# A hybrid decoder layer on one core: the gated unit of the second half woven into the first output projection, the last RWKV group split in place, and pools whose tiles wait by bytes

## The chip, the cores and the metric

The kernel runs on one core of a Trainium2 chip. The metric is the device time of one execution in microseconds. Three runs of the kernel before took 1652.79, 1653.51 and 1653.67 us; their median is 1653.51 us. One further execution was recorded by the hardware profiler, and every row quoted below is from it.

## The reference, cut to what matters

One layer of a trunk with 1024 tokens and 1024 channels, in float32. The token mixer has two branches, an RWKV-7 recurrence (8 heads of 64) and an S5 state space with a gated unit (GLU) behind it; each is projected to the model's width, gated and summed, and the sum goes through one output projection and a norm. A convolutional feed-forward part follows.

```python
h = rms_norm(x, g_mix_pre)
proj = h @ w_in                                   # RWKV columns | S5 input | two gates
gates = sigmoid(proj[..., -2048:] + b_gate)
y = wkv7_scan(...)                                # sequential over tokens
y = (group_norm(y) * lnx_w + lnx_b + bonus) * g   # RWKV branch
s = gelu(s5(u)); s = s * sigmoid(s @ w_glu + b_glu)   # S5 branch with its gated unit
mixed = (g_rwkv * (y @ w_branch_rwkv) + g_s5 * (s @ w_branch_s5)) @ w_out
x = x + rms_norm(mixed, g_mix_post)               # post norm
f = (gelu(conv(h2 @ w_gate)) * conv(h2 @ w_val)) @ w_down     # h2 = rms_norm(x, g_ffn_pre)
x = x + rms_norm(f, g_ffn_post)
```

## The kernel before

**Layout.** Everything is held transposed: channels on the 128 partitions, tokens along the row. The 1024 tokens are worked as two halves of 512 (`th` 0 and 1). A float32 product is made of three matmuls: each operand is split into a rounded high part and a rest (`split`, `split_half`, `load_w`), and `mm3_steps` issues high x high, high x low, low x high for each 128 channels of depth. Those three matmuls are called a k-step here. A weight tile comes from DRAM into one of two landing buffers (`wf`), ScalarE rounds it (`wh`, line 155) and VectorE subtracts (`wl`, line 156); four pairs are kept.

**Order.** TensorE runs in the order in which the program emits its work. The other engines' instructions are placed by Tile, a scheduler that simulates the program ahead of time and goes by priorities. The emission is planned by `drive`: it holds *lanes*, generators that yield a cost and a time to wait (`T_CH`, `T_LN`, `T_RS`, `T_N5` and so on are such waits in model microseconds), and a list `fill` of further generators that give TensorE work while the lanes wait. So the recurrence, whose steps are short and depend on one another, is a lane; projections and gate tiles are filler. Filler has the priority HPW, above the lane's HP2. `self.pause` stops the filler, `self.mark` says where `drain` shall stop.

**The recurrence.** It runs in four groups: (half 0, channel rows 0 and 1), (half 0, rows 2 and 3), (half 1, rows 0 and 1), (half 1, rows 2 and 3). For each, `chain_lane` runs `rwkv_nat`, `rwkv_level`, `rwkv_chain` (eight chunks; line 814 reads the state S, line 825 evacuates UV, line 835 updates S) and `rwkv_out`. `rwkv_out` norms the result on VectorE (lines 845 to 855), transposes it (line 861), applies weight and bias (line 863), fetches the bonus and the gate factor through the SP queue (line 867), applies them (line 868) and stores the result to the DRAM tensor YR (line 869).

**Around its end.** After the second group the filler gets `merge` (branch projections and gates of half 0) and `outproj(0)` (output projection of half 0: eight tiles of eight k-steps, with squares accumulated, lines 1174 to 1179). When the fourth group begins it also gets `merge_s5`: first the S5 outputs of half 1 are read and split, then `glu_tile` makes the four tiles of the gated unit (four k-steps each; evictions at lines 1041, 1026, 1042, 230, 231), and then eight gate tiles project them (`gate`, line 1052). Each gate tile reads its gate tensor GT through SP (line 1049). These eight gate tiles come after the recurrence.

Then `mix_out` begins with new pools. `merge_rk` reads the four rows of YR back through SP (line 1126), splits them and makes eight gate tiles (lines 1052, 1133, 230, 231), and `outproj(1)` follows. Beside them runs the lane `mid_norms(0)`: sum of squares of the first projection by TensorE (line 244), inverse root by twelve tiny VectorE operations (lines 264 and 135 to 140), spreading it over the partitions by TensorE (line 270), then the post norm on VectorE (lines 1153, 1154, 258) with x read through SP (line 1145), and 40 model microseconds later its own sum of squares.

**Pools.** On-chip buffers come from pools that are opened and closed as the program goes on; a pool that is opened later lies on bytes of pools that were closed. In this version all tiles of the new pool wait for every user of the pools whose bytes it lies on. Such changes are between S5 and RWKV (near 265 us), between the recurrence and `mix_out` (near 846 us), and before, inside and after the feed-forward part (near 965, 1065 and 1400 us).

Of the kernel before, what the change touches and what calls it, by code (L numbers as in the profile page):

```python
# [9 lines left out]
F32 = mybir.dt.float32  # L10
# [60 lines left out]
class Kern:  # L71
# [175 lines left out]
    def tm(self):  # L247
        return self.nrm.tile([128, 512], F32, tag="Tm", name=self.nm("tm"), bufs=NTM)
# [55 lines left out]
    def s5_setup(self):  # L304
# [4 lines left out]
        with self.tc.tile_pool(name="s5tmp", bufs=1) as pool:  # L309
# [528 lines left out]
    def rwkv_out(self, d):  # L838
# [3 lines left out]
        o = slice(th * 512, th * 512 + 512)  # L842
        yn = d["yn"].rearrange("p c u h i -> p (c u h) i")
# [13 lines left out]
        for u in range(2):  # L857
# [187 lines left out]
    def gate(self, j, m, th, br, t, out):  # L1045
# [3 lines left out]
        nc.sync.dma_start(t, self.GT[8 * j + m][:, th * 512:th * 512 + 512])  # L1049
# [46 lines left out]

    def merge_s5(self, first):

        s8 = (128, 8, 64)

        slots = self.slots
        xs = []
        for b in range(4):
            y = self.s5_y(self.et(s8), b, 1)
            xs.append(slots("ex", b))
            self.s5_split(*xs[b], y)
        br = []
        for m in range(4):
            br.append(slots("eb", m))
            yield from self.glu_tile(m, xs, self.et(), lambda: self.s5_y(self.et(s8), m, 1), br[m])  # L1110
        for m in range(NK):
# [6 lines left out]
            yield from self.gate(1, m, 1, br, self.et(), first[m])  # L1118

    def merge_rk(self, first, mg):  # L1120

        nc = self.nc
        br = []
        for k in range(4):
            y = self.t2()
            nc.sync.dma_start(y, self.YR[k][:, 512:1024])
            br.append([self.t2(F32R), self.t2(F32R)])
            self.split(*br[k], y)
        yield 0
        for m in range(NK):  # L1130
            t = self.t2()
            yield from self.gate(0, m, 1, br, t, t)
# [4 lines left out]
    def post_norm(self, src, ss, th, gain, resid, store, squares=None):  # L1137
# [9 lines left out]
        y = self.rstd(ss, 1e-6, 1.0 / D)  # L1147
        yield 0, T_RS
# [17 lines left out]
    def outproj(self, th, mg, mx):  # L1166

        nc, hp = self.nc, self.hp[th]
        for m in range(NK):
            w = self.load_w(self.a["w_out"][m])  # L1170
            ps = self.gmp()
# [6 lines left out]
            if m:  # L1178
                nc.vector.tensor_tensor(sq, sq, self.acc[th], ALU.add)
# [665 lines left out]
```

## Time and profile before

| | us |
|---|---|
| median of three runs | 1653.51 |
| lowest, highest | 1652.79, 1653.67 |
| span of the profiled execution | 1650.5 |
| TensorE busy in it | 1556.1 |
| VectorE busy in it | 1128.4 |
| ScalarE busy in it | 700.1 |

The profiled execution's own device time is not on its page; only its span is, from the first to the last instruction. The median of the runs lies 3.0 us above the span, so that much is taken to lie around it. Times in the rows count from the start of the span. A row of the timeline gives start, length, engine, line, operation, output and inputs, and in brackets how long the engine had been idle and what ended that. Matmuls overlap: a length of 0.39 us stands for a step of about 0.23. The granted clock is 1.00 at full speed and 0.50 when the chip halves TensorE's clock.

### The profile page before, as it was taken

The page shows a single profiled execution, that of the slowest core. Times are in us where ns is not written, and L with a number is a line of the kernel's source. Part 1 is how long each engine was busy: PE and PEld are TensorE (multiplying, and loading weights), DVE is VectorE, ACT ScalarE, POOL GpSimd, SP SyncE. Part 2 cuts the span into 40 slices and gives each one's busy share as a digit, 9 for nine tenths or more (in the row PEclk, how much of TensorE's full clock was granted, in tenths as well). Part 3 has the DMA queues.
Part 4 walks back from the last instruction along what each step waited for, and adds up shares of the span by engine and source line. Part 5 has one row for each costly group of instructions (what it writes and reads, how often), then busy time and mean ns, then how long its engine had stood idle before and what let it go on. Part 6 is the DMA issues. An engine that isn't in the chain of part 4 may idle for free.

```text
span 1650.5 us, 22688 instructions
## 1 busy us (share of the span) xinstructions
PE 1556.1 (94%) x8372; PEld 1252.4 (76%) x8372; DVE 1128.4 (68%) x2035; ACT 700.1 (42%) x1069; POOL 134.7 (8%) x190
## 2 busy tenths in 40 slices
PE   5899899899999999989999899999999999999995
PEld 4688787687787787767777688788888888788774
DVE  6898764554364365595378668977777777788667
ACT  4345443133243243546444445544444444443451
POOL 1100001312112112110000000000000000000000
PEclk9899999998997998999999899999999999999998
DMA  5344244333333334554167554322222223963632
GB/s 174 86 142 148 78 134 142 100 110 109 90 121 104 90 119 149 149 147 128 53 189 251 159 159 144 132 89 77 89 77 85 94 78 132 316 221 99 212 97 102
DMA packets 132382, 213.63 MB, mean 129 GB/s; under 512 B 38144, under 2 KB 44288, under 8 KB 132272
## 3 DMA queue, kind: packets, MB, share of 16 engines
q1 hardware_dynamic: 124208, 188.32, 36.4%
q0 software_dynamic: 6912, 21.77, 4.5%
q10 hardware_dynamic: 1152, 2.10, 0.3%
q8 instruction: 66, 1.08, 0.3%
q14 instruction: 44, 0.36, 0.1%
HBM read 156.56 MB, written 53.48 MB: 127 GB/s over the span
## 4 chain that ended last, share of the span: by engine, by line
PE 51%; DVE 8%; DMA 5%; issue 2%; ACT 1%; SPq 0%; DVEq 0%; POOL 0%; ACTq 0%
PE gm L171 5%; PE rp L1295 4%; PE rp L1296 4%; PE rp L1297 4%; PE gm L172 4%; PE gm L173 4%; DMA st<-in_w_down_dram 2%; PE mm L1295 2%; PE mm L1296 2%; PE mm L1297 2%; PE d L1470 2%; PE d L1471 2%; PE d L1469 2%; PE ch L171 1%; PE ch L172 1%
## 5 line engine op out<-in xcount | busy, mean ns | idle before, releaser
L171 PE MATMUL gm<-hh,wh 128*128 128x512 f32 x688 | 301.2, 438 | 7.6 <-ACT hh L225 3.7
L172 PE MATMUL gm<-hl,wh 128*128 128x512 f32 x688 | 278.3, 405 | 4.6 <-DVE hl L226 3.7
L173 PE MATMUL gm<-hh,wl 128*128 128x512 f32 x688 | 277.5, 403 | 0.0
L156 DVE TENSOR_TENSOR wl<-wf,wh 128x512 fp32r<-128x512 f32 x179 | 123.1, 689 | 131.1 <-ACT wh L155 129.4
L155 ACT CAST wh<-wf 128x512 fp32r<-128x512 f32 x179 | 110.9, 620 | 207.6 <-PE gm L172 125.1
L171 PEld LDWEIGHTS gm<-hh,wh 128*128 128x128 f32 x688 | 133.7, 194 | 44.4 <-ACT hh L225 5.7
L172 PEld LDWEIGHTS gm<-hl,wh 128*128 128x128 f32 x688 | 134.5, 195 | 31.7 <-DVE hl L226 6.8
L173 PEld LDWEIGHTS gm<-hh,wl 128*128 128x128 f32 x688 | 134.0, 195 | 29.7
L1470 PE MATMUL d<-xl,wh 128*128 128x512 f32 x308 | 120.8, 392 | 6.4 <-DVE xl L226 6.4
L1469 PE MATMUL d<-xh,wh 128*128 128x512 f32 x308 | 120.8, 392 | 2.1 <-ACT xh L225 2.1
L1471 PE MATMUL d<-xh,wl 128*128 128x512 f32 x308 | 120.6, 392 | 0.0
L1295 PE MATMUL rp<-t,h 128*128 128x512 f32 x216 | 84.4, 391 | 1.8 <-ACT p L1309 1.4
L1297 PE MATMUL rp<-t,l 128*128 128x512 f32 x216 | 84.2, 390 | 0.5 <-DVE l L226 0.5
L1296 PE MATMUL rp<-t,h 128*128 128x512 f32 x216 | 84.1, 389 | 0.0
L1470 PEld LDWEIGHTS d<-xl,wh 128*128 128x128 f32 x308 | 58.2, 189 | 20.2 <-DVE xl L226 8.1
L1469 PEld LDWEIGHTS d<-xh,wh 128*128 128x128 f32 x308 | 58.2, 189 | 14.5 <-ACT xh L225 2.4
L1471 PEld LDWEIGHTS d<-xh,wl 128*128 128x128 f32 x308 | 58.1, 189 | 12.1
L225 ACT CAST h<-r 128x1024 fp32r<-128x1024 f32 x34 | 35.9, 1055 | 61.1 <-PE rp L1296 32.5
L226 DVE TENSOR_TENSOR l<-r,h 128x1024 fp32r<-128x1024 f32 x34 | 41.7, 1225 | 29.2 <-ACT h L225 27.7
L1316 DVE SCALAR_TENSOR_TENSOR y<-zv,vecs,y 128x1023 f32<-128x1023 f32 (+1 forms) x36 | 46.1, 1280 | 8.6 <-ACT y L1314 8.6
L1295 PEld LDWEIGHTS rp<-t,h 128*128 128x128 f32 x216 | 40.5, 188 | 11.4 <-ACT p L1309 2.2
L1297 PEld LDWEIGHTS rp<-t,l 128*128 128x128 f32 x216 | 40.5, 188 | 9.5 <-DVE l L226 1.0
(435 smaller groups left out, 3372.5 us busy)
## 6 DMA issues: line engine op xcount, KB each, us to landing
r<-in_w_up_dram SPq DMA_DIRECT2D x36, 512.0 KB, 3.6
wf<-in_w_in_dram SPq DMA_DIRECT2D x68, 256.0 KB, 3.1
st<-in_w_down_dram SPq DMA_DIRECT2D x55, 256.0 KB, 4.2
st<-ACT SPq DMA_DIRECT2D x44, 256.0 KB, 4.8
wf<-in_w_up_dram SPq DMA_DIRECT2D x36, 256.0 KB, 2.8
ACT<-y POOLq DMA_DIRECT2D x18, 512.0 KB, 2.9
GT<-ev SPq DMA_DIRECT2D x32, 256.0 KB, 2.2
wf<-in_w_br_dram SPq DMA_DIRECT2D x32, 256.0 KB, 3.0
```

The source lines that it names most:

```text
L155: nc.scalar.copy(h[:, :n], f[:, :n])
L156: nc.vector.tensor_tensor(l[:, :n], f[:, :n], h[:, :n].bitcast(F32), ALU.subtract)
L171: mm(ps, a, xh[k], start=k == 0, stop=False)
L172: mm(ps, a, xl[k], start=False, stop=False)
L173: mm(ps, b, xh[k], start=False, stop=k == n - 1)
L1295: mm(ps, wh[:, c], xh, start=first and k == 0, stop=False, skip_group_check=True)
L1296: mm(ps, wh[:, c], xl, start=False, stop=False, skip_group_check=True)
L1297: mm(ps, wl[:, c], xh, start=False, stop=k == 3, skip_group_check=True)
L1316: V.scalar_tensor_tensor(y[:, lag:], z[:, 0:1024 - lag], self.vec(nme, i), y[:, lag:], ALU.mult, ALU.add)
L1469: mm(ps, wh[:, c], xh[:, x], start=start, stop=False, skip_group_check=True)
L1470: mm(ps, wh[:, c], xl[:, x], start=False, stop=False, skip_group_check=True)
L1471: mm(ps, wl[:, c], xh[:, x], start=False, stop=stop, skip_group_check=True)
```

## The change

- **Gated unit.** `merge_s5` loses its first part. `s5_glu` builds five generators (the inputs, and four tiles), and `out_glu`, which takes the place of `outproj(0)` in the filler, runs them between the projection's tiles: inputs and first tile after tile 3, then one after tiles 4, 5 and 7.
- **Post norm 0.** `out_glu` ends with the sum of squares and the inverse root. `mid_norms(0)` starts at the spread. For half 1 the order stays, except that x is now requested after the inverse root.
- **Last group.** In the fourth group `rwkv_out` requests the four factor tiles at its start, through the POOL queue, and splits its result straight into the operands of `merge_rk` instead of storing it to YR. `merge_rk` reads only rows 0 and 1 back, through POOL.
- **Gates.** For half 1 the gate tensors GT are read through the POOL queue.
- **Pools.** Every on-chip pool gets `reuse_waits="tile"`: a tile waits only for earlier users of its own bytes (in PSUM, of its own bank). The pools `y1p` and `nrt` are placed ahead of `nrm`, `Tm` moves to `nrt`, and NT2B goes from 25 to 15 buffers.

```diff
 def rwkv_out(self, d):
+        final = th == 1 and d["g"] == 1
+        ts = []
+        def factors(u):
+            r = []
+            for src in (d["bv"][u], self.TG[2 * d["g"] + u][:, o]):
+                t = self.tg("ld", NLD)
+                (G if final else nc.sync).dma_start(t, src)
+                r.append(t)
+            return r
+        if final:
+            ts = [factors(u) for u in range(2)]
...
-            for src, op in ((d["bv"][u], ALU.add), (self.TG[p][:, o], ALU.mult)):
-                t = self.tg("ld", NLD)
-                nc.sync.dma_start(t, src)
+            for t, op in zip(ts[u] if final else factors(u), (ALU.add, ALU.mult)):
                 V.tensor_tensor(y1, y1, t, op)
-            nc.sync.dma_start(self.YR[p][:, o], y1)
+            if final:
+                self.br[p] = self.pair(1, p)
+                self.split(*self.br[p], y1)
+            else:
+                nc.sync.dma_start(self.YR[p][:, o], y1)
 def gate(self, j, m, th, br, t, out):
-        nc.sync.dma_start(t, self.GT[8 * j + m][:, th * 512:th * 512 + 512])
+        (nc.gpsimd if th else nc.sync).dma_start(t, self.GT[8 * j + m][:, th * 512:th * 512 + 512])
+    def s5_inputs(self, xs):
+        for b in range(4):
+            y = self.s5_y(self.et(s8), b, 1)
+            xs.append(self.slots("ex", b))
+            self.s5_split(*xs[b], y)
+        yield 0
+    def s5_glu(self):
+        s8, xs = (128, 8, 64), []
+        self.br5 = [None] * 4
+        def tile(m):
+            self.br5[m] = self.slots("eb", m)
+            yield from self.glu_tile(m, xs, self.et(), lambda: self.s5_y(self.et(s8), m, 1), self.br5[m])
+        return [self.s5_inputs(xs)] + [tile(m) for m in range(4)]
+    def out_glu(self, mg):
+        for m in range(NK):
+            yield from self.outproj_tile(0, m, mg, self.mx0)
+            if self.glu and m == 3:
+                yield from self.glu.pop(0)
+            if self.glu and m in (3, 4, 5, 7):
+                yield from self.glu.pop(0)
+        ss = self.rp()
+        self.sumsq(ss, self.acc[0], True)
+        self.y0 = self.rstd(ss, 1e-6, 1.0 / D)
+        yield 0.8
 def merge_s5(self, first):
...
+        while self.glu:
+            yield from self.glu.pop(0)
...
 def merge_rk(self, first, mg):
-        for k in range(4):
+        for k in range(2):
             y = self.t2()
-            nc.sync.dma_start(y, self.YR[k][:, 512:1024])
-            br.append([self.t2(F32R), self.t2(F32R)])
-            self.split(*br[k], y)
+            nc.gpsimd.dma_start(y, self.YR[k][:, 512:1024])
+            self.br[k] = self.pair(1, k)
+            self.split(*self.br[k], y)
 def mid_norms(self, th, mx):
-        yield 0, T_N0
+        if th:
+            yield 0, T_N0
+            ss = self.rp()
+            self.sumsq(ss, self.acc[th], True)
+            yield 0.8, 0.5
+            y = self.rstd(ss, 1e-6, 1.0 / D)
+            yield 0, T_RS
+        else:
+            y = self.y0
         ss = self.rp()
-        self.sumsq(ss, self.acc[th], True)
-        yield 0.8, 0.5
-        ss, s0 = self.rp(), ss
 def build(self):
-        with tc.tile_pool(name="const", bufs=1) as self.const, ...
+        with tc.tile_pool(reuse_waits="tile", name="const", bufs=1) as self.const, ...
 def chain_lane(self, mg):
+                self.first, self.br = [], [None] * 4
+                self.glu = self.s5_glu()
...
-                self.fill += [self.merge(mg), self.outproj(0, mg, self.mx0)]
+                self.fill += [self.merge(mg), self.out_glu(mg)]
-NT2B = 25
+NT2B = 15
```

`outproj_tile` is the body of `outproj` for one tile, and `outproj(1)` calls it eight times.

More of the change, by code (lines that the diff above doesn't have):

```diff
@@ L308, in s5_setup @@
         self.s5 = s = {}
-        with self.tc.tile_pool(name="s5tmp", bufs=1) as pool:
+        with self.tc.tile_pool(reuse_waits="tile", name="s5tmp", bufs=1) as pool:
             def sm(n=32, dt=F32):
@@ L1135, in merge_rk, with post_norm @@
             self.split_half(*mg[m], t)
-    def post_norm(self, src, ss, th, gain, resid, store, squares=None):
+    def post_norm(self, src, y, th, gain, resid, store, squares=None):
         nc = self.nc
```

96 lines of the change are left out of this document (44 added, 52 removed).

## The prediction

> **What bounds the kernel now.** I read the page first, then the busy table in stretches of 10 us, then TensorE's timeline where it sat idle, then the chain of waits and the queues around those places.
>
> ```profile
> span 1650.5 us, 22688 instructions
> PE 1556.1 (94%) x8372; PEld 1252.4 (76%) x8372; DVE 1128.4 (68%) x2035; ACT 700.1 (42%) x1069; POOL 134.7 (8%) x190
> ```
>
> ```profile
> 780.00:790.00 10.00, 10.00 (x83) 7.40 (x82) 3.26 (x8) 4.79 (x12) 0.00 (x0) 1.00 0.16 52
> ...
> 840.00:850.00 10.00, 7.74 (x32) 5.44 (x31) 8.17 (x12) 7.58 (x14) 0.00 (x0) 1.00 0.87 247
> ...
> 845.30:961.30 116.00, 103.77 (x419) 81.94 (x418) 81.57 (x146) 46.76 (x81) 0.00 (x0) 0.90 0.63 197
> ```
>
> The columns are the stretch, its length, busy PE, PEld, DVE, ACT, POOL, the granted clock, DMA share, GB/s. TensorE is the bound: full before the recurrence ends (780 to 790), with holes after it. From 845.3 to 961.3 it is idle 116 - 103.8 = 12.2 us, and a mean clock of 0.90 means 0.10 x 2 x 116 = 23 us at half speed, so up to 11.6 us more are lost.
>
> The same loss counted from the work:
>
> ```profile
> 845.28 0.39 PE L173 MATMUL gm<-e,wl 128*128 128x512 f32 x1
> 883.63 0.79 PE L171 MATMUL mm<-t,wh 128*128 128x512 f32 x1 [3.31 <-ACT t L225]
> 895.70 0.39 PE L171 MATMUL mm<-t,wh 128*128 128x512 f32 x1
> 901.14 0.39 PE L171 MATMUL mm<-t,wh 128*128 128x512 f32 x1
> 915.22 0.80 PE L171 MATMUL mm<-t,wh 128*128 128x512 f32 x1 [3.61 <-ACT t L230]
> 918.62 0.80 PE L171 MATMUL mm<-t,wh 128*128 128x512 f32 x1 [1.39 <-ACT t L230]
> 961.14 0.39 PE L171 MATMUL mm<-hh,wh 128*128 128x512 f32 x1
> 963.86 0.95 PE L244 MATMUL rp<-ones,sq 128*128 128x1 f32 x8
> ```
>
> 895.70 and 901.14 are eight k-steps (three matmuls each) apart: 0.68 us a step. The last gated unit's matmul starts at 845.28, the second output projection is over at 961.14. Between them stand 16 gate tiles of 4 steps, 8 projection tiles of 8, two sums of squares and two spreads of about 0.9 us: 128 x 0.68 + 3.6 = 90.6 us of 115.5. So 23 to 25 us are lost; I use 24. What ended the waits:
>
> ```profile
> 857.35 3.07 DMA YR<-ld
> 872.07 4.82 DMA wf<-in_w_br_dram
> 878.74 4.20 DMA t<-YR
> 911.07 5.40 DMA t<-GT
> ```
>
> The last RWKV result goes out to YR and comes back (line 1126), the last reload issued only at 878.74, because SP issues in order and weights and x stand ahead of it. The last gate tile t<-GT is issued at 911.07 for the same reason, when the projection already waits for it.
>
> **The change, part by part.**
>
> *Group split in place.* It removes two stores and two reloads of YR, and brings the bonus and gate factors early. The wait of 3.31 us goes, with its half-speed stretch. Two splits of rows 2 and 3 (about 0.7 us each on VectorE) move ahead of 846. They write buffers that the first projection still reads, so they wait for its last step, about 843 in the new order; nothing needs them before the ninth gate tile, some 22 us later.
>
> *Gates on the POOL queue.* Sixteen loads leave SP. POOL is idle there (0.00 in each row above), and in the second half nothing but the two YR reloads and the four factor loads shares its queue. The 3.61 and 1.39 us waits, which hang on t<-GT, should go.
>
> *Gated unit woven in.* The amount of filler work is unchanged, so the recurrence ends where it did:
>
> ```profile
> 825.09 0.40 PE L832 MATMUL chb<-UV,bkn 128*64 128x64 f32 x5
> ```
>
> From 825 on 28 steps of filler remain in either order: before, 12 of the projection and 16 of the unit; now one and a half projection tiles lie behind unit tiles, and only the fourth unit tile (4 steps) comes last. Three of four evictions are then over before the gates want them. Cover for the fourth is priced with the next part.
>
> *Post norm 0.* The sum of squares and the inverse root now stand at the end of the filler, and the spread is the next thing that TensorE is given. Before, 4 us of filler (T_RS) lay between them. So TensorE waits for the 12 tiny VectorE operations:
>
> ```profile
> PE d L270 <- DVE rsy L140: 2.4, 1, 2.4
> ```
>
> ```profile
> 855.87 0.16 DVE L264 TENSOR_SCALAR rv<-rp 128x4 f32<-128x4 f32 x1 [0.21 <-PE rp L244]
> 862.58 0.16 DVE L140 SCALAR_TENSOR_TENSOR rsy<-rsh,rsy 128x4 f32<-128x4 f32 x1
> ```
>
> 2.4 us is the wait where this pair stands back to back already (the last norm); 6.7 us is what the same operations took here before, stuck behind others on VectorE. I take 3.5, nearer the first, since the 2.9 us wait for a YR store inside the 6.7 is gone. The fourth unit tile's eviction hides under it: 0.68 + 1.07 + 0.63 + 0.69 = 3.1 us, from
>
> ```profile
> L1041 ACT ACTIVATE et<-gm,hb_b_glu x4: 682/683/685, 837.0 to 846.0; 128x512 f32<-128x512 f32 x4
> L1042 DVE SCALAR_TENSOR_TENSOR et<-et,et x4: 1051/1057/1094, 841.8 to 850.6; 128x512 f32<-128x512 f32 x4
> 851.70 0.63 ACT L230 ACTIVATE e<-et 128x512 fp32r<-128x512 f32 x1 [1.13 <-DVE et L1042]
> 852.37 0.69 DVE L231 SCALAR_TENSOR_TENSOR e<-et,e 128x512 fp32r<-128x512 f32 x1 [0.70 <-ACT e L230]
> ```
>
> The post norm's own sum of squares is issued a fixed 40 us (T_N5) of filler behind the spread, now without holes in between:
>
> ```profile
> 863.70:910.10 46.40, 43.09 (x178) 34.78 (x177) 40.60 (x66) 19.58 (x33) 0.00 (x0) 0.93 0.78 252
> 909.36 0.69 DVE L258 TENSOR_TENSOR tm<-tm,tm 128x512 f32<-128x512 f32 x1
> 910.67 0.95 PE L244 MATMUL rp<-ones,tm 128*128 128x1 f32 x8
> ```
>
> VectorE needed 40.6 busy us for this, and was done 0.6 us before TensorE asked. It now has 40. With the two splits off it, 39.2 busy us at its present 88% take 45: a wait of 0 to 5 us, and I take 3. The projection's last operand and the second spread have the same VectorE behind them: 0 to 2, I take 1. Each of these waits can cost half speed for one or two stretches of 3.4 us, 1.7 to 3.4 us lost; I count two at 1.5, since some will trip nothing.
>
> Beside the recurrence the unit's evictions now stand on VectorE and ScalarE among the chain's. The first half does the same already:
>
> ```profile
> 689.20 0.50 PE L828 MATMUL chk<-UV,gr 128*64 128x64 f32 x5 [0.54 <-DVE UV L825]
> ```
>
> That wait, the longest there, cost 0.54; I take 1 for all four tiles, with an upper end in the last rival. Sum here: 24 - 3.5 - 3 - 1 - 3 - 1 = **12.5 us** (from 22 if only 2.4 is paid, to -1.5 if all upper ends are: 6.7 + 5 + 2 + 6.8 + 5).
>
> By the Trainium skill (TensorE: Matmul & The Clock Gate, Part 1) half speed follows at least one idle window of about 3.4 us, so waits of 2.4 to 3.5 us would mostly trip nothing and the sum would be some 3 us better. The 2.05 us wait at 1408 below, followed by a stretch at 0.50, speaks against it, so the sum keeps them.
>
> *Waits by bytes.* Its work hides in the changes of pools. Between S5 and RWKV:
>
> ```profile
> 268.66 0.62 ACT L751 COPY x<-csts 128x512 f32<-128x512 f32 x1 [0.69 <-DMA YU<-t]
> 268.92 1.80 POOL L725 MEMSET UV<- 64x2048 f32 x1 [38.51 <-DVE wl L156]
> 270.70 0.50 PE L171 MATMUL gm<-hh,wh 128*128 128x512 f32 x1 [3.16 <-DVE ev L919]
> 272.00:276.00 4.00, 4.00 (x12) 3.13 (x11) 1.02 (x1) 2.01 (x2) 0.62 (x1) 0.57 0.97 314
> ```
>
> POOL had nothing for 38 us, and ACT, POOL and TensorE all start when the last YU store has landed or the last evacuation is done: a barrier. The new accumulator lies most likely over an S5 bank freed by 266, so 3.16 us and half of 3.4 us go: 0 to 4.9, I take 4. At the down projection:
>
> ```profile
> 1408.26 0.47 PE L1469 MATMUL d<-xh,wh 128*128 128x512 f32 x1 [2.05 <-ACT xh L225]
> 1408.80:1412.20 3.40, 3.40 (x9) 2.64 (x8) 3.40 (x4) 0.59 (x1) 0.00 (x0) 0.50 1.01 349
> ```
>
> The second operand pair waits for all users of the feed-forward operands, though its own bytes come free some steps earlier: 2.05 + 1.7, so 0 to 3.8, I take 2. Inside the feed-forward change I take 0.5 (-1 to 1). Together **6.5 us**.
>
> Total 19 us. The profiled execution's span goes from 1650.5 to 1631.5; the runs' median lies 3.0 above the span, so **1634.5 us**.
>
> **The rivals.**
>
> *Full cover:* root and post norm find VectorE free and no half speed follows. Only 2.4 + 1 is lost, 20.6 + 6.5 = 27: 1626 or, with all of the barriers' 9.7, 1623. Against it: VectorE at 40.6 of 46.4.
>
> *Data arrive too slowly:* gates, x, stores and weights meet in 44 us (846 to 890) instead of 64 (to 910), and wf already took 4.82 us there.
>
> ```profile
> L156 DVE TENSOR_TENSOR wl<-wf,wh 128x512 fp32r<-128x512 f32 x179 | 123.1, 689 | 131.1 <-ACT wh L155 129.4
> L155 ACT CAST wh<-wf 128x512 fp32r<-128x512 f32 x179 | 110.9, 620 | 207.6 <-PE gm L172 125.1
> ```
>
> With these and two landing buffers a weight tile takes (4.82 + 0.62 + 0.69) / 2 = 3.07 us, against 4 x 0.68 = 2.72 on TensorE. Sixteen tiles lose 5.6 us where the lead of four tiles doesn't cover it, and post norm 0, which shares VectorE, slips a further 3: 1643. By the Trainium skill (SBUF — State Buffer, on the three doors) VectorE operations in a two-port mode keep GpSimd from writing descriptors, which would put the POOL-queue gates late in just this stage. As a mechanism here: one late gate at the end costs 3.61 + 1.39 and about 3.5 of half speed as before, again 1643. Against it stands the landing of the stores that POOL issues while VectorE is full:
>
> ```profile
> ACT<-t POOLq DMA_DIRECT2D x8, 256.0 KB, 2.7
> ```
>
> *The pools' waits don't relax:* if Tile can't follow a pool's users it keeps the old barrier; the 6.5 us stay lost, 1641.
>
> *Slower:* the woven unit delays the recurrence. One mechanism: its evictions, which have priority over the chain's, stand ahead of UV and S on VectorE and ScalarE from 800 on. If no part is hidden, four tiles cost 4 x 3.7 us (the eviction's 3.1 and the gelu's 0.63) = 14.8, and four stalls of that size each bring a half-speed stretch worth 3 us: 26.8 against a gain of 19 + 1: 1660. It decides from about 5 us a tile. Against it: 0.54 us in the first half, and VectorE busy 3.26 of 10 at 780.
>
> **How the numbers follow.** Forecast 0.50, full cover 0.14, slow data 0.15, no relaxed waits 0.12, slower 0.06, nothing 0.03. A change of 0.2% (3.3 us) is what these runs can tell from none. All of the first four but a tail of 0.04 are faster: 0.87; the tail and the last case give 0.06 for the same, and 0.07 is slower. The range reaches into full cover and past slow data: 1620 to 1648; the forecast's own is 1628 to 1641.
>
> **What would show it.** Right: no wait for YR or GT in the chain of waits; TensorE's idle time between the unit's end and the second projection's end near 8 us instead of 12, and one or two half-speed stretches; a wait of 2.4 to 4 us at line 270 there; TensorE busy through the pool change near 267. Wrong: new waits on S L835 or UV L825 while the unit is woven in; gate matmuls waiting for wh; a wait above 5 us at the post norm's sum of squares; POOL-queue loads landing after 5 us or more.

## The result, and the profile after

| | before | after |
|---|---|---|
| time, median of 5 runs beside each other | 1653.67 us (1652.79 to 1656.39) | 1644.27 us (1638.70 to 1647.22) |
| ratio, 95% interval | | 0.9945 (0.9924 to 0.9966) |
| span of the profiled execution | 1650.5 us | 1645.4 us |

The change gains 9.4 us (5.6 to 12.6 by the interval). The forecast was 1634.5, a gain of 19: right in sign, twice too large. The profiled execution of after is the slowest of its five, so its rows show less of a gain than the median. Its own time is 1647.22 us, 1.8 above its span; in the other four executions of after 1.8 to 2.5 us lie around the span, so the 3.0 that the forecast adds is about 1 us too much. In two later comparisons on other chips the ratio was 0.9942 (0.9924 to 0.9960) and 0.9956 (0.9941 to 0.9971).

The first lines of the page of after:

```profile
span 1645.4 us, 22661 instructions
...
PE 1552.2 (94%) x8372; PEld 1251.5 (76%) x8372; DVE 1129.1 (69%) x2035; ACT 701.0 (43%) x1069; POOL 146.2 (9%) x212
```

TensorE is still the bound. Line numbers are each kernel's own: 861 before is 873 after. Three marks in TensorE's timeline of before that the prediction did not show, in S5, at the last group's transposes and behind the gated unit's last matmul:

```profile
225.32 0.46 PE L613 MATMUL chk<-t,ca 128*128 128x128 f32 x2 [2.23 <-DVE t L607]
732.81 0.90 PE L861 MATMUL rp<-csts,yn 128*128 128x128 f32 x3 [5.64 <-DVE yn L855]
...
846.74 0.50 PE L171 MATMUL mm<-e,wh 128*128 128x512 f32 x1 [1.07 <-ACT et L1041]
```

And TensorE's timeline of after at its marks and waits:

```profile
226.96 0.46 PE L613 MATMUL chk<-t,ca 128*128 128x128 f32 x2 [2.21 <-DVE t L607]
...
285.44 0.47 PE L171 MATMUL gm<-hh,wh 128*128 128x512 f32 x1 [3.24 <-DVE last L935]
...
734.36 0.90 PE L873 MATMUL rp<-csts,yn 128*128 128x128 f32 x3 [5.80 <-DVE yn L867]
...
767.25 0.69 PE L786 MATMUL chk<-gr,ld 32*32 32x32 f32 x16 [2.46 <-ACT gr L788]
...
853.13 1.05 PE L244 MATMUL rp<-ones,sq 128*128 128x1 f32 x8 [0.44 <-DVE sq L1214]
857.19 2.05 PE L270 MATMUL rp<-csts,rsy 128*128 128x128 f32 x8 [3.01 <-DVE rsy L140]
...
910.07 1.13 PE L270 MATMUL rp<-csts,rsy 128*128 128x128 f32 x8 [1.36 <-DVE rsy L140]
...
918.15 0.50 PE L171 MATMUL mm<-t,wh 128*128 128x512 f32 x1 [4.24 <-ACT t L230]
...
963.57 0.61 PE L244 MATMUL rp<-ones,sq 128*128 128x1 f32 x5
...
1405.70 0.39 PE L1513 MATMUL d<-xh,wh 128*128 128x512 f32 x1
```

The waits for YR (3.31) and GT (3.61 and 1.39) are gone, and so are the 3.16 us at the S5 change and the 2.05 us at the down projection. New are 3.24 at 285, 2.46 at 767 and 3.01 at 857; the 4.24 at 918 stands where 3.61 stood, before the projection's last operands. The busy table of after, columns as in the prediction:

```profile
770.00:845.00 75.00, 75.00 (x525) 56.83 (x523) 31.48 (x68) 34.09 (x72) 0.55 (x1) 0.97 0.25 71
...
852.70:961.00 108.30, 97.16 (x417) 79.10 (x418) 76.20 (x138) 44.53 (x76) 5.42 (x10) 0.95 0.59 187
...
1405.70:1409.10 3.40, 3.40 (x17) 2.81 (x16) 3.40 (x5) 3.35 (x5) 0.00 (x0) 1.00 0.52 172
```

Beside the recurrence (770 to 845) TensorE shows no idle time although the unit is woven in. Behind the unit it now idles 11.1 us (108.30 - 97.16) where the prediction read 12.2 before, and loses 5.4 by half speed (0.05 x 108.3) against 11.6. The down projection begins at full speed.

Between the marks, gains in us. The second pair are one profile each of the two kernels from the experiments, spans 1652.2 and 1639.6:

| stretch | forecast | first pair | second pair |
|---|---|---|---|
| start to 225 | 0 | -1.6 | -0.1 |
| to the transposes near 733 | +4 | +0.1 | +0.9 |
| to the unit's end | -1 | -5.5 | -1.9 |
| to the second projection's end | +13.5 | +7.3 | +8.6 |
| to the down projection, and to the end | +2.5 | +4.8 | +5.1 |
| span | 19 | 5.1 | 12.6 |

For example the third row of the first pair: before, 846.74 - 1.07 - 732.81 = 112.86; after, 853.13 - 0.44 - 734.36 = 118.33. The first row is chance: before's second profile passed the same S5 row at 227.41. In the third profile of after the stretch to the unit's end took 118.40, and the one behind it 111.88 against 118.2 in both profiles of before.

### The profile page after: what moved, and what is told of

It is laid out like the page before. It is cut to its first block, busy times and chain, and to the rows that moved or that the text cites. A ratio compares the mean times of both kernels' runs of the same rounds, so it can differ in the third digit from the quotient of the medians.

```text
span 1645.4 us, 22661 instructions
## 1 busy us (share of the span) xinstructions
PE 1552.2 (94%) x8372; PEld 1251.5 (76%) x8372; DVE 1129.1 (69%) x2035; ACT 701.0 (43%) x1069; POOL 146.2 (9%) x212
```

## The experiments

Each edit is on the changed kernel unless it says otherwise, and leaves no work out. Ratios are to runs of the kernel before on the same chip. Executions of one kernel differ by 2 to 16 us here, so an effect under about 4 us is not settled by the times alone and is read from the waits. The split in place and the gates on POOL were not undone by themselves; what each is worth alone is not measured.

**The two kernels again.** No edit: `e_before_again` is the kernel before, `e_after_again` and `e_after_third` the changed one.

> The kernel before, profiled once more, to see which of its rows stand in every execution. In the changed kernels of the first comparison TensorE reached the same place of S5 (225 us in the first profile of before) 1.6 to 2.9 us later, with 17.1 us of half speed near 35 in place of 10.2. If that belongs to the chip or to chance, this profile shows 227 to 228 there too; if it belongs to the change, 225 again. The gated unit should end some 113 us after the transposes near 733, and the second projection 118 us later.

> The changed kernel once more, beside the three edits of it below, so that each is read against it on one chip. Both theories: 7 to 12 us faster than the kernel before (ratio 0.993 to 0.996), since the first comparison gave 9.4. In its profile the wait of some 2.5 us near 767, the one of some 3 us before the spread near 857 and the one of some 4 us near 918 should be there again; if one of them is missing, it belongs to that one execution and not to the change.

> The changed kernel a third time, as the partner of the run beside it on the same chip: 0.9935 to 0.9955 of before by its first two comparisons (0.9945 and 0.9942). The root's wait of 3.01 us and the last operand's of 4.24 us should be there again; the wait near 766 between 1.0 and 2.5 us.

Measured: 1654.29 us for the one execution of before; 1641.38 (0.9942) and 1644.56 (0.9956) for the changed kernel. The late start stood in before's second profile too (227.41), so it is no part of the change. The waits 3.01 before the spread and 3.80 to 4.25 at the last operand stood in all three profiles of after, the one near 766 with 1.32 to 2.60; half speed followed it in two of three. The second spread waited 1.36, 0.84 and 3.35.

**What the waits by bytes are worth.** Taken out of the changed kernel (`e_no_bytes`), and put alone into the one before (`e_bytes_only`); the order on every engine is unchanged.

```diff
-tc.tile_pool(reuse_waits="tile", name=..., ...)    # e_no_bytes, all pools
+tc.tile_pool(name=..., ...)
```

> All pools wait as before again; the order of every engine is the changed kernel's. The prediction gave these waits 6.5 us, 4 of them between S5 and RWKV. Theory from the two traces: only the down projection's wait of 2.05 us and its half speed come back, 4 to 5 us; between S5 and RWKV the 3.2 us come back near 270 but the 3.24 us near 285 go, net within 1 us, because there the first group's loads and not the pools set the time. So 4 to 5 us slower than the changed kernel. Rival: the prediction's sum holds and the new wait near 285 has another cause (the woven order, or chance): then it stays, and the kernel is 6 to 9 us slower than the changed one. If both traces' differences are only chance, it is within 2 us.

> The kernel before with nothing but the waits by bytes, all other code and every engine's order as before. With pool waits put back, the changed kernel lost its whole gain (ratio to before 1.0009, interval 0.9994 to 1.0024). Theory: the waits by bytes are nearly all of the gain, in either order of the work; then this kernel is 7 to 11 us faster than before (0.9933 to 0.9958). Rival, the prediction's sum: 6.5 us (0.996), with the S5 wait near 270 worth 4 of them. Second rival: the changed order made new pool waits of its own (1.92 us near 1071, 2.25 us near 910 in that run), so that they cost more there than here; then this kernel gains only 3 to 5 us, the down projection's part.

Measured: without them 1652.51 us, 1.0009 (0.9994 to 1.0024): the whole gain is gone, 11.2 us on the mean of the changed kernel beside it (9.4 to 13.0). Alone in the old order 1646.99, 0.9974 (0.9960 to 0.9988): 4.3 us. So the parts don't add up: the new order without byte waits gains nothing that these runs can tell, byte waits alone gain 4.3, and both together 7 to 10. Between the two profiles of the changed order, 9.1 us apart, 4.9 lie from the second projection's end to the down projection, 2.5 between the unit's end and the second projection's end, and 1.7 ahead of that. TensorE's timeline without them:

```profile
272.89 0.50 PE L171 MATMUL gm<-hh,wh 128*128 128x512 f32 x1 [3.16 <-DVE ev L933]
...
910.37 0.79 PE L270 MATMUL rp<-csts,rsy 128*128 128x128 f32 x5 [2.25 <-DVE rsy L140]
...
1070.69 0.50 PE L1339 MATMUL rp<-t,h 128*128 128x512 f32 x1 [1.92 <-ACT h L225]
...
1409.28 0.47 PE L1513 MATMUL d<-xh,wh 128*128 128x512 f32 x1 [2.06 <-ACT xh L225]
```

So the rival with pool waits of the new order holds: 1.92 us at the feed-forward change is a wait that the kernel before didn't have, and byte waits cut it to 0.7 to 0.9 and remove the old 2.06. The 3.16 near 273 came back and the wait near 285 went: one replaces the other.

**Why S5 to RWKV gained nothing.** The first group's six loads on POOL's queue.

```diff
-k, tz, ta = (ld(x) for x in (...))
+k, tz, ta = (ld(x, nc.sync if d["g"] or d["th"] else G) for x in (...))
```

> The changed kernel with one edit: the first RWKV group's six loads of k, decay and a (RKV, TZ, TA) go to the POOL queue. The prediction gave 4 us to the S5-to-RWKV change of pools; the traces show the wait of 3.16 us near 270 gone and one of 2.0 to 3.6 us near 285 (line 171, released by line 935 on VectorE) in its place. Theory: these loads still start at 270.8, because SP reaches them only behind a weight load that waits for its buffer until 270.4, in either kernel; their first use on ScalarE (line 662) stands ahead of the evictions in ScalarE's queue, so TensorE's wait only moves. With the loads free of SP the front starts some 3 us earlier, the wait near 285 shrinks to under 1 us, and the kernel is 2 to 4 us faster than the changed one, whose ratio is 0.9942. Rival: the front's own chain (13 us from its loads to the wait of 5.0 us at line 700) is what counts, and that chain starts from the S5 results, not the loads: then line 700 is reached at the same time and the total is within 1.5 us.

Measured: 0.9956 (0.9940 to 0.9971), no gain. In its timeline of TensorE the wait near 285 is another one, and line 700 is no earlier (78.6 us behind the S5 mark; 78.0 to 80.3 in the three profiles of after):

```profile
286.52 0.90 PE L683 MATMUL rp<-csts,gr 128*128 128x128 f32 x3 [3.18 <-ACT gr L681]
...
303.62 0.76 PE L700 MATMUL rp<-ar,bk 64*128 64x128 f32 x2 [3.35 <-DVE gr L702]
```

From the S5 mark at 224.99 to the transposes it took 507.47 us, as in the first pair (507.49 and 507.40). The loads' place was not the bound, so my theory fell; that the front's own chain is, as the rival has it, fits these rows, but no run shortened that chain.

**Is weaving worth its price?** The unit behind the projection again.

```diff
-if self.glu and m == 3: yield from self.glu.pop(0)
-if self.glu and m in (3, 4, 5, 7): yield from self.glu.pop(0)
```

> The changed kernel with the second half's gated unit behind the first projection again; the split in place, the gates on POOL, the root at the projection's end and the waits by bytes stay. Prediction's view: weaving hides the fourth unit tile's eviction and two waits (1.07 and 1.05 us in the profile of before, with 6.8 us at half speed), at a price of 1 us beside the recurrence; undone, 3 to 5 us are lost. Rival: since the root and the spread now have 11 us of unit work between them, the 3.01 us wait before the spread goes, and its half speed; the two waits of the last unit tile come back in its place, and the kernel is within 2 us of the changed one: weaving only moves the wait. If the small wait near 766 (1.0 to 2.5 us in the profiles so far) comes from weaving, it goes too.

Measured: 1648.42 us, 0.9988 (0.9975 to 1.0001); against 0.9942 to 0.9956 some 5 to 8 us are lost, more than the 3 to 5 expected. The prediction's view, that weaving pays, holds. Its timeline of TensorE:

```profile
840.37 0.83 PE L244 MATMUL rp<-ones,sq 128*128 128x1 f32 x6 [3.59 <-DVE sq L1214]
...
859.59 0.50 PE L171 MATMUL mm<-e,wh 128*128 128x512 f32 x1 [1.92 <-ACT e L230]
860.73 0.50 PE L172 MATMUL mm<-e,wh 128*128 128x512 f32 x1 [0.65 <-DVE e L231]
862.99 0.79 PE L171 MATMUL mm<-e,wh 128*128 128x512 f32 x1 [1.52 <-ACT e L230]
```

The spread's wait is gone, but the sum of squares, now right behind the last projection tile, waits 3.59 for that tile's square and sum, and the unit's third and fourth tiles are late as operands, by 2.6 and 1.5. The wait near 766 (1.37) stays: it isn't weaving's.

**The wait near 766.** The last group's four factor loads on SP at their use; on ScalarE's queue at about 838; and the S5 output loads put ahead of them on POOL.

```diff
-(G if final else nc.sync).dma_start(t, src)    # issued at the head of rwkv_out
+nc.sync.dma_start(t, src)                      # e_late_factors, at the products
+(A if final else nc.sync).dma_start(t, src)    # e_factors_act, behind the root of the group norm
-self.nc.sync.dma_start(t, self.YU[b]...)       # e_yu_pool
+(self.nc.gpsimd if th else self.nc.sync).dma_start(t, self.YU[b]...)
```

> The last RWKV group's four bonus and gate loads go back to SP, at the place of their use; the split in place stays. Theory: the wait of 2.46 us near 767 and the 3.4 us lost to half speed behind it come from these four loads of 256 KB, which POOL issues at 745.5 to 747.2, 90 us before their use, and which hold up the S5 outputs (YU, 9.6 us to landing against 4.5 before) that stand first in ScalarE's queue. Then the S5 outputs land in about 4.5 us again, the wait near 767 is gone, and the kernel is 4 to 6 us faster than the changed one. Rival: the wait comes from the weaving itself, since the inputs of the second half's unit now stand at another place of the filler: then the wait near 767 stays at 2 to 3 us whatever the factor loads do, and the time is within 2 us of the changed kernel's. A loss elsewhere: the factors, now behind weights on SP, come late for the last group's products near 847, which would show as a wait of the ninth gate tile or of the spread.

> The changed kernel with the last group's four factor loads issued by ScalarE's queue just before their use (about 837 to 841), neither early on POOL nor behind weights on SP. Theory: the early POOL issue makes the wait near 766 (1.0 to 2.5 us, with 0 to 6.8 us of half speed), and the place on SP made the waits of 3.98 and 3.48 us near 852. Here neither is there: the wait near 766 is gone, the sum of squares waits under 1 us, and the kernel is 1 to 5 us faster than the changed one (0.9918 to 0.9940 where that is 0.9942 to 0.9950). Rival: ScalarE's queue, 0.35 us for each issue, delays the unit's evictions, or the factors land after 847; then a wait of 2 us or more stands before the sum of squares as in the SP version.

> The changed kernel with the second half's eight S5 output loads (YU) on the POOL queue, where the first four stand ahead of the four factor loads of the last group, and the last one no longer behind weights on SP. Theory: the wait near 766 (1.0 to 2.5 us wherever the factor loads stand on POOL, none with them on SP or in the kernel before) comes from these factor loads reaching the DMA engines ahead of the YU loads; with the order turned round it goes to under 0.5 us. And the fourth unit tile's operand, late by 0.3 + 0.7 us now and by 4.77 us once the spread was put 4 us later, comes earlier. Gain 1 to 3 us on the changed kernel. Rival: the DMA engines are full there whoever comes first; then weights come late instead and the wait near 766 stays.

In after, POOL's issues, ScalarE's queue, and the landing of the S5 outputs issued from 742 to 757 (KB each, median us):

```profile
745.51 0.59 POOL L850 DMA_DIRECT2D ld<-bv  x1
...
747.18 0.55 POOL L850 DMA_DIRECT2D ld<-TG  x1
```

```profile
757.33 0.63 ACT L1040 ACTIVATE et<-et 128x512 f32<-128x512 f32 x1 [4.33 <-DMA et<-YU]
```

```profile
et<-YU SPq DMA_DIRECT2D x2, 256.0 KB, 9.6
```

In the kernel before, in the same stretch:

```profile
et<-YU SPq DMA_DIRECT2D x4, 256.0 KB, 4.5
```

ScalarE stands still 4.33 us for them, and what lies behind in its queue, line 788 among it, comes late. With the factor loads on SP or on ScalarE's queue there is no wait near 766 (TensorE 13.00 of 13.00 us busy from 757 to 770 with the latter), so the cause is shown. The stretch from the transposes to the unit's end is then 113.4 us on SP and 112.9 on ScalarE's queue, against 112.9 and 112.8 before and 114.7 to 118.4 in the changed kernel: all that this stretch lost came with the early loads, and the weaving itself cost 0 to 0.6. It can't be had back for nothing: on SP the time is 1647.02, 0.9970 (0.9953 to 0.9987). There they land late, and the last sum (line 1214) stands behind their products (line 878) on VectorE, so that the sum of squares waits 3.98 and the spread 3.48:

```profile
848.25 1.42 DVE L878 TENSOR_TENSOR ld<-ld,ld 128x512 f32<-128x512 f32 x2 [2.99 <-DMA ld<-TG]
...
851.22 0.68 DVE L1214 TENSOR_TENSOR sq<-sq,sq 128x512 f32<-128x512 f32 x1
```

On ScalarE's queue the time is 1639.15, 0.9943 (0.9921 to 0.9965), no different from the changed kernel. There the root's wait grew to 5.55, TensorE and VectorE:

```profile
852.55 2.05 PE L270 MATMUL rp<-csts,rsy 128*128 128x128 f32 x8 [5.55 <-DVE rsy L140]
```

```profile
847.04 0.16 DVE L264 TENSOR_SCALAR rv<-rp 128x4 f32<-128x4 f32 x1 [1.15 <-PE rp L244]
849.66 0.69 DVE L156 TENSOR_TENSOR wl<-wf,wh 128x512 fp32r<-128x512 f32 x1 [2.46 <-ACT wh L155]
850.27 0.16 DVE L135 TENSOR_SCALAR rsy<-rv 128x4 int32<-128x4 int32 x1
```

Between the first and the second of the root's operations of 0.16 us stands a weight split that waits 2.46 us for its cast: 3.0 + 2.5. The same 2.5 stood in `e_first_pool` (5.56), where the factor loads were still on POOL, so it is how the weight stream falls, not the factor loads as such. With YU on POOL the wait near 766 grew to 3.86 and the time to 0.9984 (0.9973 to 0.9995). POOL's second YU load waited 3.37 us for its buffer, and the loads behind it with it. ScalarE waits for no S5 output there, so these come in time; but lines 788 and 785 stand behind gelus and casts in ScalarE's queue and run only at 767.4 and 767.9, and TensorE waits for the latter. The gain that I expected failed on that order.

**The root's wait.** The 4 us of filler put back before the spread; and the sum, root and spread among the gate tiles with the fourth unit tile earlier.

```diff
+y = self.y0; yield 0, T_RS                 # e_spread_late
-if self.glu and m in (3, 4, 5, 7):
+if self.glu and m in (3, 4, 5, 6):         # e_root_gates
-if th: yield 0, T_N0; ss = ...; else: y = self.y0
+yield 0, T_N0; ss = ...                    # both halves as half 1; out_glu's own sum and root go
```

> The changed kernel with the 4 us of filler (T_RS) between the root and the spread of post norm 0 put back, nothing else. Theory: the 3.01 us wait at line 270 and the 3.4 us of half speed that starts with it in every profile of the changed kernel are what the back-to-back place costs, 3 + 1.7; with the gate tiles in between, the spread doesn't wait, but the fourth operand of the first gate tile, whose eviction the wait hid, is late by 1 to 3 us in its place. Net 1 to 3 us faster than the changed kernel. Rival: the fourth operand's lateness takes the whole place, and the post norm, issued 4 us later, delays the second spread and the last operand: same time or up to 3 us slower.

> Half 0's sum of squares, root and spread go back to where they stood before, among the first gate tiles (2.5 us of filler, sum, 4 us of filler, spread), and the fourth unit tile is woven in one projection tile earlier. Theory: the 3.01 us wait before the spread is there in every profile of the changed kernel, and filling it alone only uncovered the fourth unit tile's eviction (4.77 us); with that tile ahead of the last projection tile both are covered, so that no wait over 1 us and no half speed stand between 845 and 865: 3 to 6 us faster than the changed kernel. Rival: the root takes 6.7 us here as before, since VectorE is full of gate products, and the wait for the spread comes back as 2 to 3 us; then no gain.

Measured: 0.9952 (0.9933 to 0.9970) and 0.9951 (0.9934 to 0.9968), no gain from either. With the spread later, TensorE's and ScalarE's timelines:

```profile
855.03 0.79 PE L171 MATMUL mm<-e,wh 128*128 128x512 f32 x1 [4.77 <-ACT e L230]
```

```profile
852.62 0.63 ACT L1040 ACTIVATE et<-et 128x512 f32<-128x512 f32 x1 [4.02 <-DMA et<-YU]
```

The fourth unit tile takes the whole place, and not for its 3.1 us of eviction alone: its S5 output lands 4.02 us after ScalarE wants it, SP having issued it behind weights. With all three among the gate tiles the spread waits again, 3.75 us at 865: the root's last operations stand behind a split that waits 2.58 us for ScalarE.

**The last operand.** The second norm 10 us later; 4.8 us of sums off VectorE; products ahead of weight splits.

```diff
-T_N5 = 40.0
+T_N5 = 50.0                                          # e_norm_late, e_norm_prod
-self.nc.vector.tensor_tensor(sq, sq, acc, ALU.add)
+self.nc.gpsimd.tensor_tensor(sq, sq, acc, ALU.add)   # e_acc_light
+with self.tc.high_priority(2 * HPW): ...             # e_norm_prod: lines 1066, 1171, split
```

> One constant: the post norm's own sum of squares of half 0 stands 50 us of filler behind the spread instead of 40, and the second norm with it. Theory: the wait of 4.24 us near 918 (and 1.36 for the second spread, 0.34 and 0.75 beside it, and about 3.4 us by half speed behind them) comes from VectorE's order: the first products and splits of the second norm stand ahead of the last gate tile's product, so 3 to 4 us of them delay the projection's last operand. With the second norm 10 us later the 4.24 and the 1.36 go, and the kernel is 6 to 10 us faster than the changed one. Rival: VectorE is full there from 863 to 924 whatever the order, so the gate tile's product is late anyway: then a wait of 2 us or more at the last operand stays, and the gain is under 3 us. Second rival: the gate values land late; then nothing changes.

> The changed kernel with the seven sums of squares of post norm 0 (line 258, 0.69 us each on VectorE) on POOL. The wait of 4.25 us at the second projection's last operand near 914 was 2.92 with the second norm moved away; VectorE is busy without a gap from 863 to 924 there. Theory: it is VectorE's total load, so taking 4.8 us off it cuts the last operand's wait to under 1.5 us and with it 3.4 us of half speed: 3 to 6 us faster than the changed kernel (0.9942). Rival: it is the order alone, the second norm's first products ahead of the last gate product: then the wait stays at 3 us or more, since the order is kept. Loss: POOL's sums stand between the gate loads on its queue, so late gates (more than 6 us from issue to use) would show as waits of VectorE for GT.

> The version with the second norm 10 us later, and the gate products, sums and splits of the second projection's operands ahead of the weight splits in VectorE's order where both are free. The wait at the last operand was 4.25 us, 2.92 + 0.76 with the norm later, 3.91 with 4.8 us of sums taken off VectorE. Theory: what is left is VectorE's order, each product standing behind a weight split that waits for a buffer until TensorE frees it; with products first the wait falls under 2 us and the kernel is 1 to 3 us faster than with the later norm alone (ratio 0.9938). Rival: what is left is the chain itself, four operations on two engines for each of the last tiles, 4.0 us a tile against 2.7 on TensorE; then the wait stays at 2.5 to 3.5 us and the time is the same.

VectorE's timeline of after, where line 1066 is the gate product, 1171 its sum, 231 the split, 1247 and 226 the second norm:

```profile
909.84 0.68 DVE L1066 SCALAR_TENSOR_TENSOR t<-t,mm 128x512 f32<-128x512 f32 x1
...
911.77 0.74 DVE L1247 SCALAR_TENSOR_TENSOR tm<-mx,vecs,rp 128x512 f32<-128x512 f32 x1
...
914.95 0.68 DVE L226 TENSOR_TENSOR hl<-tm,hh 128x512 fp32r<-128x512 f32 x1
915.55 0.68 DVE L1066 SCALAR_TENSOR_TENSOR t<-t,ch 128x512 f32<-128x512 f32 x1
```

The last gate tile's matmuls end at 906.0, its product runs at 915.55. The expected 6 to 10 us did not come. With the second norm later (1640.24 us, 0.9938, 0.9919 to 0.9958; against 1641.38 beside it not settled), TensorE and VectorE:

```profile
908.48 0.50 PE L171 MATMUL mm<-t,wh 128*128 128x512 f32 x1 [2.92 <-ACT t L230]
```

```profile
901.33 0.68 DVE L1066 SCALAR_TENSOR_TENSOR t<-t,ch 128x512 f32<-128x512 f32 x1
...
905.38 0.68 DVE L1066 SCALAR_TENSOR_TENSOR t<-t,mm 128x512 f32<-128x512 f32 x1
...
907.08 0.69 DVE L1171 TENSOR_TENSOR t<-t,e 128x512 f32<-128x512 f32 x1
908.46 0.69 DVE L231 SCALAR_TENSOR_TENSOR t<-t,t 128x512 fp32r<-128x512 f32 x1 [0.70 <-ACT t L230]
909.07 0.68 DVE L1066 SCALAR_TENSOR_TENSOR t<-t,ch 128x512 f32<-128x512 f32 x1
```

So the second norm in front cost 1.3 us of the longest wait here and the second spread's 1.36. What is left fits the rival's chain: product, sum, ScalarE, split. VectorE stands idle 0.70 for ScalarE ahead of the next product, and the last three products come 3.7 to 4.1 us apart, against 2.72 a tile on TensorE. Less load does little (3.91 left, 0.9961, 0.9947 to 0.9976), products first little too (2.57 + 1.25, 0.9953, 0.9935 to 0.9971). But the latter did not keep the weight splits out of the way, as VectorE's timeline of `e_norm_prod` shows:

```profile
902.08 0.69 DVE L156 TENSOR_TENSOR wl<-wf,wh 128x512 fp32r<-128x512 f32 x1 [1.24 <-ACT wh L155]
902.68 0.69 DVE L1171 TENSOR_TENSOR t<-t,e 128x512 f32<-128x512 f32 x1
```

So the chain of a tile and the weight splits between its operations have not been told apart; that part of the wait, some 3.7 us, is open.

**Edits together.** `e_all5`: later norm, sums on POOL, YU on POOL, first loads on POOL, filler before the spread. `e_root_act`: root among the gates and factor loads by ScalarE. `e_act_norm`: factor loads by ScalarE and later norm.

> Five edits together on the changed kernel: the second norm of half 0 10 us later, its sums of squares on POOL, YU loads on POOL, the first RWKV group's six loads on POOL, and the 4 us of filler between root and spread put back. If the waits found so far are what the missing half of the forecast went into, TensorE loses little between the unit's end and the second projection's end: waits under 3 us in all and one stretch of half speed, and the kernel is 7 to 12 us faster than the changed one (0.987 to 0.990 of before). If what one edit gives another takes back, as with the spread alone, it is within 4 us of it (0.992 to 0.995).

> The two edits of this call together: factor loads by ScalarE's queue, and sum of squares, root and spread among the gate tiles with the fourth unit tile earlier. If both theories hold the gains add up: 4 to 10 us faster than the changed kernel (0.988 to 0.992 of before). If each only moves its wait to the last operand of the second projection, whose operations on VectorE then come later too, it is within 3 us of the changed kernel.

> The changed kernel with the two edits that did what they were made for and took nothing back: the last group's factor loads by ScalarE's queue (no wait near 766) and the second norm of half 0 10 us later (the last operand's wait 2.9 + 0.8 us in place of 4.25 + 0.75 + 1.4). If they add up, this is 2 to 5 us faster than the changed kernel beside it, 0.990 to 0.993 of before. If the root's wait grows again to 5.55 us, as it did with the factor loads on ScalarE's queue alone, the two are the same within 2 us.

Measured: 0.9972 (0.9955 to 0.9989), 0.9938 (0.9920 to 0.9956), 0.9938 (0.9916 to 0.9961). Nothing adds up. The last, 1641.41 us, is 3 us under the changed kernel beside it (1644.56), which seven and twelve executions don't settle; its spread waits 5.42. No version clearly beats the changed kernel.

## Why the prediction was right in sign and wrong in size

Three steps failed. The projection's last operand and the second spread, priced at 1 us, lost 6.7 (5.9 and 7.9 in the other two profiles of after). The pool change between S5 and RWKV, priced at 4 us of gain, gave 0.1 to 0.9. The early factor loads, priced at nothing, cost 1.9 to 5.6 us in the stretch that ends with the unit. Half speed behind the unit, priced at 3, cost 5.1. The other way went the post norm's own sum, priced at 3 and free, and the feed-forward part with the down projection, which gave about twice its 2.5.

*Group split in place, gates on POOL:* right in that no wait for YR or GT is left. But TensorE did not get back the 3.61 + 1.39 us that hung on GT: at the same place, the projection's last operands, it now waits 4.24 + 0.75 for something else. The gate loads issued from 863 to 910 in after (KB each, median us to landing), and that stretch's busy row:

```profile
t<-GT POOLq DMA_DIRECT2D x4, 256.0 KB, 5.8
et<-GT POOLq DMA_DIRECT2D x4, 256.0 KB, 6.2
```

```profile
863.00:910.00 47.00, 45.26 (x202) 37.23 (x202) 40.67 (x76) 17.36 (x30) 4.24 (x8) 1.00 0.71 230
```

They took over the 5 us that the prediction set as a mark of failure, with VectorE busy 40.67 of 47, but were issued far enough ahead: nothing waited for one. By the Trainium skill (SBUF — State Buffer, on the three doors) they could have starved beside VectorE operations in a two-port mode. No run here shows whether the operations of this stage use that mode, so the prediction's step from a busy VectorE to late gates stays unproven. POOL's queue was not as empty as the prediction says: in the last group four stores and four loads of the recurrence (xd) stand on it at 737 to 745, ahead of the factor loads. What the step left out is the price of the early factor loads: 1 to 2.6 us near 766, at times 3.4 more by half speed. It said that they come "early" and asked nothing of what they pass.

*Gated unit woven in, 1 us lost beside the recurrence:* the term measured 5.5 and 1.9, but by those loads: without them it is 0 to 0.6. TensorE waits for nothing from 770 to 845, and weaving itself is worth 5 to 8 us. The slower rival has no row for it.

*Post norm 0, wait before the spread 3.5:* measured 3.01, and 5.4 to 5.6 where a weight split falls in between. Right. That the fourth unit tile hides under it was right in the changed kernel (0.3 + 0.7 us remain).

*Its own sum of squares 3, last operand and second spread 1:* the two terms were the wrong way round. The sum waited 0; the operand and the spread lost 4.24 + 0.75 + 0.34 + 1.36 = 6.7 us. This is the step that failed most. I reckoned VectorE's busy share and let every operation wait alike. The sum's operands are early: the last is done near 892.8, and TensorE wants it at 901.5. The last operand's product stands behind the second norm, worth 1.3 us of it and the spread's 1.36; the rest fits a chain of four operations per tile with weight splits in between, and is open.

*Half speed 2 x 1.5:* 3.4 and 6.8 us at half speed in the section cost 1.7 + 3.4 = 5.1.

Together the section gained 7.3 and 8.6 in the two pairs where 13.5 was said, 4.9 to 6.2 less. In the first pair the terms account for 6.7 - 1 - 3 = 2.7 at the operand and the sum, 5.1 - 3 = 2.1 by half speed, 1.0 at the fourth tile, 0.4 at the first sum and -0.5 at the root: 5.7.

*Waits by bytes, 6.5:* the sum hid two errors. S5 to RWKV, 4 us said, gave 0.1 to 0.9, because the wait only went from 270 to 285. What it hangs on there is open: earlier loads did not move it. The feed-forward and down projection, 2.5 said, gave 4.8 to 5.1 in the rows, and 11.2 went in all when the bytes were undone, in part because the new order has a pool wait of its own.

The time lies beside two rivals' figures (1643, 1641) by chance, since neither mechanism is there: pools do relax, and gates and weights came in time; the late data were the S5 outputs, which no rival named.

## What to carry to other kernels

A transfer moved to an idle queue starts as soon as its buffer is free, so ask what it meets at that moment, not when it is used. When a wait is removed, find the next instruction behind it in each in-order queue before counting its length as gain: here the same 3 us went from 270 to 285, and from the spread to the fourth tile. For the last of a row of tiles count its chain of operations across engines and what stands between them, not the busy share of one. Undo each part in the new order as well as adding it to the old one: the byte waits were worth 4.3 us in the one and 11.2 in the other.

## What was not expected of the hardware

Half speed also came where the trace shows TensorE busy throughout, and not in every execution. Twenty us from the same wait at line 783, first in after, then in its third profile:

```profile
502.40:522.90 20.50, 20.48 (x147) 15.65 (x147) 7.45 (x27) 7.62 (x13) 3.89 (x6) 0.59 0.48 154
```

```profile
504.46 0.69 PE L783 MATMUL chb<-ld,gr 32*32 32x32 f32 x16 [1.81 <-DVE ld L781]
...
504.40:524.90 20.50, 19.86 (x200) 15.62 (x201) 12.78 (x35) 9.49 (x18) 5.71 (x8) 1.00 0.51 166
```

The clock is 0.59 in the one and 1.00 in the other after waits of 1.80 and 1.81 us. From this row to the transposes after took 231.9 us and its third profile 224.9, so 7.0 us of a run's time hang on it. The other 19 profiles of this case all have 13.7 or 17.1 us at half speed there. By the Trainium skill (TensorE: Matmul & The Clock Gate, Part 1) the window of activity is about 3.4 us and runs free of the kernel. The stretches at half speed, but for the last of each trace, are 3.4, 6.8, 10.2, 13.7 or 17.1 us long, which agrees with such a window; that its place in time is what differs between executions fits, but no run shows it. By the same part of the Trainium skill half speed takes at least one idle window; that does not agree, since 2.46 us at 767 were enough in after. The length of a wait does not decide it either: 3.24 us at 285 brought none there, and 3.09 us at the same row brought 6.8 us in the third profile.
